# All of the planner's free choices to VectorE, and an early call for the first two attention weights

## The chip, the cores and the metric

The kernel runs on one core of a Trainium2 chip. The metric is the device time of one execution in microseconds. The engines are named as the profile names them: PE is TensorE (PEld its weight loads), DVE is VectorE, ACT is ScalarE, POOL is GpSimd, SP is SyncE, which only issues DMAs here. Times of the kernel before: 2492.51 us, median of three runs (2489.13 to 2495.65).

## The reference

One layer of a decoder trunk serves a prompt of 512 tokens and 8 samples of 8 new tokens each with the same weights, all in float32. Cut to what matters:

```python
proj = x @ w_in
u, cq, ckv_raw, kr_raw = jnp.split(proj, [1024, 1536, 2048], axis=-1)
y_ssm, h_last = s5_group(u, h0, p)                       # state scan, then GLU
q = (rms_norm(cq, g_q) @ w_uq).reshape(b, s, 8, 192)     # 128 plain + 64 rotary per head
q_lat = einsum('bshn,rhn->bshr', q[..., :128], w_uk)
q_rope = apply_rope(q[..., 128:], pos)
ckv, krope = rms_norm(ckv_raw, g_kv), apply_rope(kr_raw, pos)
o_lat = attend(q_lat, q_rope, ckv, krope)                # causal, or over 1024 cached rows
y_att = einsum('bshr,rhv->bshv', o_lat, w_uv)
x = layer_norm(alpha * x + concat([y_ssm, y_att]) @ w_out)
x = layer_norm(alpha * x + (silu(x @ w_gate) * (x @ w_up)) @ w_down)
```

## The kernel before, in words

All 576 tokens (512 of the prompt, 64 of the samples) are the moving columns of the matmuls, in two halves of 288. Weights and activations are split into a high part, rounded to a shorter format, and a low part, the rest; a product is three matmuls: high by high, high by low, low by high (`mm3`, `mmx`). A split (`split`) is a copy to the high part on ACT and a subtraction for the low part on DVE or POOL. So each weight that PE uses passes a DMA, ACT and then DVE or POOL; `wraw`, `whi` and `wlo` are its three tiles. `Ring` loads and splits the weights in the order of a list, two ahead; `weights` makes the list that begins with the prompt attention, and its first two entries are the value and key halves of `w_kv`.

The stages: the input projection with the S5 parameters, states, taps and state scan beside it (`in_proj`, `s5_side`; to about 312 us); the first queries (`to_heads`, `rope_queries`, `nope_queries`) and the prompt attention (`prompt_phase`, to about 500); the sample attention over the cached pages together with the output projection, the residual sums `z` and the first layer norm (`sample_phase`, `out_phase`, `norm1`); the FFN, whose gate, up and most of whose down products use a form of fast matrix multiplication with 7 products for 8 (`ffn_phase`; from about 890); the second layer norm (`norm2`) on the last sums.

A layer norm of one half runs in three steps. `shift` subtracts a rough mean from each of 16 blocks `z`; `moments` adds up blocks and squares (the accumulators lie in `m`, `QS` or, in the last norm, in `xl`); `normed` takes pairs of blocks, 576 columns, subtracts the mean, multiplies by the reciprocal deviation, and scales and shifts each block on ACT or DVE, whichever the planner holds free earlier.

The order of the instructions on each engine is made while the program is built. The class `Clock` keeps a planned end time for every engine and tile, the generators (fibers) of the stages are advanced by these times (`merge`), and a scheduler then orders the instructions by priority (`cur_priority`) and its own timeline. `sooner` is the place where the plan chooses between DVE and POOL for one elementwise operation: it takes POOL where the planned end there is more than 500 ns before the planned end on DVE. It serves the low parts of `split` from SBUF, the sums of `rope`, the low parts of the rotary queries, the low parts of the cached pages (`pages`: `ckthi` and `cktlo` for scores, `cknlo` for values), and `shift`, `moments` and `normed`. Some work is written for POOL outright and stays there: the taps' powers `P` and `PX` and the states' products `Gx`, `Gy` in the S5 stage, copies of query columns, the sum of high and low part in `gates`, and DMAs that accumulate into `pa`.

Of the kernel before, what the change touches and what calls it, by code (L numbers as in the profile page):

```python
# [162 lines left out]
class Clock:  # L163
# [98 lines left out]

    def sooner(self, op, out, *ins):

        t = self.ready(*ins)
        d, p = (max(t + 150, self.end[e]) + self.cost(e, op, out, ins) for e in ('DVE', 'POOL'))
        return self.gpsimd if p + 500 < d else self.vector

    def note(self, eng, op, a, k, r):
        aps = [x for x in list(a) + list(k.values()) if hasattr(x, 'tensor') and hasattr(x, 'dtype')]  # L270
# [249 lines left out]
class Layer:  # L520
# [228 lines left out]
    def weights(self):  # L749

        io = self.io
        cut = lambda w: [w[:, :1024], w[:, 1024:]]
        items = []
        for pr in range(4):
            kv = cut(io['w_kv'][pr])
            lat = cut(io['w_ukt'][pr // 2])[pr % 2:pr % 2 + 1]
            items += cut(io['w_uq'][pr])[::-1] + kv[:1] + lat + kv[1:] if pr else kv[::-1] + lat
        items += [io['w_glu'][m] for m in range(8)]
        mix = [[cut(io['w_out'][m])[i] for m in range(KD)] for i in range(2)]
        items += mix[1] + mix[0]  # L760
        for m in range(8, KD):
            if m in VALUES:
                items.append(io['w_kv'][VALUES.index(m)][:, 1024:])
            items.append(mix[0][m])
        items += mix[1]
        for n in range(2 * HEADS):
            items += [io['w_gu'][n // 2, n % 2, 2 * r:2 * r + 2, :, :512].rearrange("q p c -> p q c") for r in range(2)]
        self.ring = Ring(self, self.wst, "w", 1024, items, ahead=100)

    def place(self, j):  # L770

        j -= 16
        if j < 2:
            return None
        if j == 2:
            hi, lo = self.ff.tile([128, 1024], F32R, name="E"), self.cst.tile([128, 1024], F32R, name="rp")
            return [[x[:, 256 * i:256 * i + 256] for x in (hi, lo)] for i in range(4)]
        if j == 3:
            return [list(x) for x in zip(self.t4[:4], self.t4[4:])]
        a, b = (('T2', 'B22'), ('B11', 'B21'))[j // 2 - 2]  # L780
        k = j % 2 * 2
        return self.X[a][k:k + 2] + self.X[b][k:k + 2]
# [1673 lines left out]
```

## Time and profile before

| | us |
|---|---|
| median of three runs | 2492.51 (2489.13 to 2495.65) |
| profiled execution, its own time | 2493.54 |
| its span, first to last instruction | 2491.5 |
| PE busy | 2350.2 (94%) |
| DVE busy | 1957.2 (79%), 3313 instructions |
| ACT busy | 1077.4 (43%), 1685 instructions |
| POOL busy | 444.4 (18%), 390 instructions |
| mean granted clock of PE | 0.969 |

An engine's busy time is the time covered by its instructions; two that overlap by their pipeline are not counted twice. A granted clock of 1.00 is 2.4 GHz and 0.50 is 1.2 GHz; a mean between them tells which share of a stretch ran at the lower level. In the timeline, idle time ahead of an instruction stands in brackets with what ended it.

### The profile page before, as it was taken

How to read it: one execution, taken by the hardware profiler on the slowest of the kernel's cores; microseconds unless marked ns; L12 is line 12 of the kernel's file. 1: busy time of each engine (PE TensorE's matmuls, PEld its weight loads, DVE VectorE, ACT ScalarE, POOL GpSimd, SP SyncE). 2: the span in 40 equal slices, each digit the busy share in tenths (PEclk: the TensorE clock that was granted, in tenths of full speed). 3: DMA queues.
4: the chain of work that ended last, by engine and by line, in shares of the span. 5: the costliest groups of instructions: out<-in, count | busy, mean ns of one | idle time of the engine just before them, and what ended most of it. 6: DMA issues, size and time to landing. Idle time of an engine off the chain costs nothing.

```text
span 2491.5 us, 45005 instructions
## 1 busy us (share of the span) xinstructions
PE 2350.2 (94%) x17220; PEld 2297.1 (92%) x17220; DVE 1957.2 (79%) x3313; ACT 1077.4 (43%) x1685; POOL 444.4 (18%) x390
## 2 busy tenths in 40 slices
PE   8988989999899989999999999999999999979995
PEld 7877989998898989999999999999999999979994
DVE  7759766778778886999988878887778876755978
ACT  4221355656555544433333333333336644553133
POOL 2682010143344550000000000000000000000335
PEclk9988999999999989999999999999999999989997
DMA  6563456478765556455433333333236765677622
GB/s 216 178 183 120 105 161 199 144 240 294 243 194 165 198 172 217 174 183 190 164 113 132 120 113 132 112 123 107 107 113 208 254 186 143 170 205 251 243 94 76
DMA packets 219161, 419.90 MB, mean 169 GB/s; under 512 B 62210, under 2 KB 127106, under 8 KB 217154
## 3 DMA queue, kind: packets, MB, share of 16 engines
q1 hardware_dynamic: 187154, 359.66, 43.5%
q10 hardware_dynamic: 30064, 44.98, 5.0%
q0 software_dynamic: 1728, 12.39, 2.8%
q8 instruction: 135, 2.21, 0.4%
q14 instruction: 80, 0.66, 0.1%
HBM read 337.52 MB, written 83.64 MB: 169 GB/s over the span
## 4 chain that ended last, share of the span: by engine, by line
PE 56%; DVE 12%; DMA 11%; issue 3%; ACT 3%; POOL 1%; SPq 0%; ACTq 0%; DVEq 0%; POOLq 0%
PE mm L180 34%; PE sc L180 21%; DVE wlo L180 3%; DVE z L180 2%; DVE xl L180 2%; DMA wraw<-w_gu 2%; DMA hraw<-hd 1%; PE po L180 1%; DMA cktraw<-ckt 1%; DMA mraw<-so 1%; DVE T L180 1%; ACT whi L180 1%; DMA T<-pa 1%; DVE Al L180 1%; DVE g L180 1%
## 5 line engine op out<-in xcount | busy, mean ns | idle before, releaser
L180 PE MATMUL mm<-xh,whi 128*128 128x288 f32 x2272 | 606.1, 305 | 17.5 <-ACT xh L180 9.6
L180 PE MATMUL mm<-xh,wlo 128*128 128x288 f32 x2272 | 607.1, 304 | 13.6 <-DVE wlo L180 13.3
L180 PE MATMUL mm<-xl,whi 128*128 128x288 f32 x2272 | 605.7, 303 | 4.5 <-DVE xl L180 4.0
L180 PEld LDWEIGHTS mm<-xh,whi 128*128 128x128 f32 x2272 | 409.8, 193 | 26.8 <-ACT xh L180 10.9
L180 PEld LDWEIGHTS mm<-xh,wlo 128*128 128x128 f32 x2272 | 410.6, 193 | 20.9 <-DVE wlo L180 18.0
L180 PEld LDWEIGHTS mm<-xl,whi 128*128 128x128 f32 x2272 | 411.1, 193 | 7.8 <-DVE xl L180 5.0
L180 PE MATMUL sc<-z,whi 128*128 128x288 f32 x1470 | 350.8, 297 | 1.2 <-ACT z L180 0.6
L180 ACT ACTIVATE whi<-wraw 128x1024 fp32r<-128x1024 f32 (+2 forms) x159 | 173.8, 1094 | 281.1 <-PE mm L180 187.2
L180 DVE TENSOR_TENSOR wlo<-wraw,whi 128x1024 fp32r<-128x1024 f32 (+2 forms) x150 | 214.4, 1431 | 89.7 <-ACT whi L180 87.4
L180 ACT ACTIVATE whi<-E 128x1024 fp32r<-128x1024 f32 x120 | 127.2, 1060 | 334.7 <-issue 193.1
L180 PEld LDWEIGHTS sc<-z,whi 128*128 128x128 f32 x1470 | 250.7, 189 | 2.3 <-ACT whi L180 1.0
L180 ACT ACTIVATE whi<-rp 128x1024 fp32r<-128x1024 f32 x120 | 127.4, 1061 | 256.9 <-issue 191.3
L180 DVE TENSOR_TENSOR wlo<-E,whi 128x1024 fp32r<-128x1024 f32 x120 | 146.7, 1223 | 94.0 <-ACT whi L180 93.5
L180 POOL DMA_DIRECT2D pa<-m x6 | 5.3, 890 | 1200.2 <-ACT m L180 1200.2
L180 PE MATMUL mm<-T,H 128*128 128x288 f32 x1200 | 217.3, 296 | 1.8 <-ACT T L180 1.7
L180 DVE TENSOR_TENSOR wlo<-rp,whi 128x1024 fp32r<-128x1024 f32 x120 | 146.5, 1221 | 72.1 <-ACT whi L180 71.9
L180 PEld LDWEIGHTS mm<-T,H 128*128 128x128 f32 x1200 | 180.8, 189 | 2.5 <-ACT T L180 2.2
L180 PE MATMUL mm<-Ah,wlo 128*128 128x288 f32 x480 | 137.5, 308 | 14.6 <-DVE wlo L180 12.7
L180 PE MATMUL sc<-Ah,H 128*128 128x288 f32 x552 | 144.3, 297 | 6.6 <-DVE H L180 3.2
L180 PE MATMUL mm<-Ah,H 128*128 128x288 f32 x552 | 144.4, 297 | 4.2 <-ACT Ah L180 4.2
L180 PE MATMUL sc<-z,wlo 128*128 128x288 f32 x490 | 145.8, 298 | 0.9 <-DVE wlo L180 0.9
L180 PE MATMUL sc<-g,whi 128*128 128x288 f32 x490 | 144.8, 295 | 0.9 <-ACT g L180 0.8
(505 smaller groups left out, 5493.6 us busy)
## 6 DMA issues: line engine op xcount, KB each, us to landing
wraw<-w_gu SPq DMA_DIRECT2D x145, 512.0 KB, 3.2
qns<-w_gu SPq DMA_DIRECT2D x59, 512.0 KB, 3.3
wraw<-w_out SPq DMA_DIRECT2D x56, 512.0 KB, 3.9
wraw<-w_dq SPq DMA_DIRECT2D x43, 512.0 KB, 3.4
cktraw<-ckt SPq DMA_DIRECT2D x64, 320.0 KB, 4.5
cknraw<-ckn SPq DMA_DIRECT2D x64, 256.0 KB, 3.9
hd<-QS ACTq DMA_DIRECT2D x16, 1008.0 KB, 4.1
wraw<-w_in SPq DMA_DIRECT2D x14, 1024.0 KB, 5.8
```

What stands on the lines that cost most here:

```text
L180: r = f(*a, **k)
```

## The change

`sooner` no longer compares; it returns DVE. And behind the weight list of the prompt attention, the ring is asked at once to load and split its first two entries, with a priority that is moved 400 ahead of the place reached.

```diff
     def sooner(self, op, out, *ins):
 
-        t = self.ready(*ins)
-        d, p = (max(t + 150, self.end[e]) + self.cost(e, op, out, ins) for e in ('DVE', 'POOL'))
-        return self.gpsimd if p + 500 < d else self.vector
+        return self.vector
...
         self.ring = Ring(self, self.wst, "w", 1024, items, ahead=100)
 
+        at = self.tc.cur_priority
+        self.tc.cur_priority = max(at - 400, 0)
+        self.ring.split(1)
+        self.tc.cur_priority = at
```

What this makes of the order is seen in three places. The first is ACT where the first queries end and the prompt attention begins. `rt` and `qrh` are rotary parts of the first queries, `qnh` their plain parts, `kr` the rotary key; `whi<-wraw` twice is the pair of weights. Before:

```order
L180 ACTIVATE rt<-mm 32x576 x4
L180 ACTIVATE qnh<-mm 128x576
L180 ACTIVATE kr<-rva 128x576
L180 DMA o_kr<-rva 64x576
L180 ACTIVATE qnh<-mm 128x576
L180 ACTIVATE qrh<-qr 64x576 x4
L180 ACTIVATE whi<-wraw 128x1024 x2
```

The same place now:

```order
L180 ACTIVATE rt<-mm 32x576 x4
L180 ACTIVATE qnh<-mm 128x576
L180 ACTIVATE kr<-rva 128x576
L180 DMA o_kr<-rva 64x576
L180 ACTIVATE qnh<-mm 128x576
L180 ACTIVATE qrh<-qr 64x576 x4
L180 ACTIVATE whi<-wraw 128x1024 x2
```

Nothing moved there: the pair follows the four copies `qrh` in both.

The second place is DVE where the first norm of the second half has its statistics (`RECIPROCAL QS`) and the first FFN weights are split beside it; `g` and `z` are the pairs of blocks, `QS` holds mean and reciprocal deviation. Before:

```order
L180 RECIPROCAL QS<-QS 96x3
L180 TENSOR_TENSOR wlo<-wraw,whi 128x1024
L180 TENSOR_TENSOR xres<-xres,mm 128x288
L180 TENSOR_TENSOR z_10035<-z_10035,QS 128x576 x2
L180 TENSOR_SCALAR z_10035<-z_10035,vec 128x288
L180 TENSOR_TENSOR wlo<-wraw,whi 128x1024
L180 TENSOR_TENSOR xl_212<-z_10035,xh_196 128x576
```

Now:

```order
L180 RECIPROCAL QS<-QS 96x3
L180 TENSOR_TENSOR wlo<-wraw,whi 128x1024
L180 TENSOR_TENSOR xres<-xres,mm 128x288
L180 TENSOR_TENSOR g_7372<-g_7372,QS 128x576
L180 TENSOR_TENSOR z_10035<-z_10035,QS 128x576
L180 TENSOR_TENSOR g_7373<-g_7373,QS 128x576
L180 TENSOR_TENSOR z_10036<-z_10036,QS 128x576
L180 TENSOR_TENSOR g_7372<-g_7372,QS 128x576
L180 TENSOR_TENSOR z_10035<-z_10035,QS 128x576
L180 TENSOR_TENSOR g_7373<-g_7373,QS 128x576
L180 TENSOR_TENSOR wlo<-wraw,whi 128x1024
```

Seven of the eight pairs were POOL's with both steps and came to DVE; seven steps now stand ahead of the next low part `wlo`, where two stood.

The third place is DVE at the end of the program, from the last reciprocal on; `xh_26921` holds the second half's mean and deviation, `xh_26917` the first half's. Before:

```order
L180 RECIPROCAL xh_26923<-xh_26923 96x3
L180 TENSOR_SCALAR Ah_26659<-Ah_26659,vec 128x288 x2
L180 TENSOR_TENSOR z_26646<-z_26646,xh_26921 128x576
L180 TENSOR_TENSOR z_26648<-z_26648,xh_26921 128x576
L180 TENSOR_TENSOR Al_26656<-Al_26656,xh_26921 128x576
L180 TENSOR_TENSOR z_26646<-z_26646,xh_26921 128x576
L180 TENSOR_TENSOR g_26650<-g_26650,xh_26921 128x576
```

Now:

```order
L180 TENSOR_TENSOR Ah_26657<-Ah_26657,xh_26917 128x576
L180 TENSOR_TENSOR z_26646<-z_26646,xh_26921 128x576
L180 TENSOR_TENSOR z_26648<-z_26648,xh_26921 128x576
L180 TENSOR_TENSOR g_26650<-g_26650,xh_26921 128x576
L180 TENSOR_TENSOR z_26652<-z_26652,xh_26921 128x576
L180 TENSOR_TENSOR Al_26654<-Al_26654,xh_26921 128x576
L180 TENSOR_TENSOR Al_26656<-Al_26656,xh_26921 128x576
L180 TENSOR_TENSOR Al_26658<-Al_26658,xh_26921 128x576
L180 TENSOR_TENSOR Al_26660<-Al_26660,xh_26921 128x576
L180 TENSOR_TENSOR Ah_26659<-Ah_26659,xh_26917 128x576
L180 TENSOR_TENSOR z_26646<-z_26646,xh_26921 128x576
L180 TENSOR_TENSOR z_26648<-z_26648,xh_26921 128x576
```

The differences of all eight pairs of the second half now stand on DVE ahead of their products, with late steps of the first half's pairs `Ah` around them; five of the differences were POOL's.

## Rows read from the trace of the kernel before

**Rows 1.** Stretches: us, busy us of PE, PEld, DVE, ACT, POOL, clock, DMA

```profile
500.00:880.00 380.00, 356.87 (x2426) 337.83 (x2425) 303.07 (x460) 212.38 (x333) 171.96 (x125) 0.95 0.68 222
880.00:935.00 55.00, 44.96 (x306) 44.25 (x305) 47.54 (x51) 26.07 (x41) 29.39 (x19) 0.88 0.53 173
935.00:1870.00 935.00, 930.25 (x6971) 926.89 (x6970) 776.02 (x1194) 350.36 (x456) 0.00 (x0) 1.00 0.40 140
2305.00:2430.00 125.00, 120.62 (x894) 118.86 (x893) 108.13 (x164) 31.20 (x58) 45.70 (x33) 1.00 0.46 167
2430.00:2491.50 61.50, 31.04 (x204) 29.57 (x203) 51.94 (x77) 21.63 (x45) 31.59 (x19) 0.76 0.23 77
```

**Rows 2.** PE's waits, whole span: us in total, times, longest

```profile
PE mm L180 <- DVE wlo L180: 26.0, 17, 6.9
...
PE mm L180 <- POOL P L180: 7.9, 3, 5.1
```

**Rows 3.** DVE by form, 935 to 1870 us: count, busy us, mean ns, idle before

```profile
L180 DVE TENSOR_TENSOR wlo<-E,whi 128x1024 fp32r<-128x1024 f32 x87 | 106.4, 1223 | 65.0 <-ACT whi L180 64.5
...
L180 DVE TENSOR_TENSOR QS<-QS,mm 128x576 f32<-128x576 f32 x35 | 26.2, 749 | 4.4 <-PE mm L180 4.1 <-issue 0.2
```

**Rows 4.** DVE by form, 500 to 935 us

```profile
L180 DVE TENSOR_TENSOR wlo<-wraw,whi 128x1024 fp32r<-128x1024 f32 x77 | 109.0, 1416 | 24.7 <-ACT whi L180 24.3
...
L180 DVE TENSOR_TENSOR z<-z,mm 128x288 f32<-128x288 f32 x24 | 10.7, 447 | 10.0 <-PE mm L180 10.0
```

**Rows 5.** DVE by form, 880 to 935 us

```profile
L180 DVE TENSOR_TENSOR wlo<-wraw,whi 128x1024 fp32r<-128x1024 f32 x12 | 19.0, 1582 | 6.1 <-ACT whi L180 6.1
L180 DVE TENSOR_SCALAR g<-g,vec 128x288 f32<-128x288 f32 x5 | 6.0, 1222 | 0.0
...
L180 DVE TENSOR_TENSOR z<-z,QS 128x576 f32<-128x576 f32 x2 | 3.4, 1715 | 0.1
L180 DVE TENSOR_TENSOR m<-g,z 128x576 f32<-128x576 f32 x2 | 2.7, 1352 | 0.0
```

**Rows 6.** POOL by form, 500 to 935 us

```profile
L180 POOL TENSOR_TENSOR ckthi<-cktraw,ckthi 64x256 fp32r<-64x256 f32 x30 | 41.6, 1389 | 60.7 <-ACT ckthi L180 49.2 <-PE mm L180 4.5 <-PE po L180 4.2
...
L180 POOL TENSOR_TENSOR g<-g,QS 128x576 f32<-128x576 f32 x8 | 16.2, 2040 | 8.6 <-ACT QS L180 8.6
...
L180 POOL TENSOR_TENSOR z<-z,QS 128x576 f32<-128x576 f32 x6 | 10.1, 1699 | 0.0
```

**Rows 7.** Timeline of DVE near 917 us: start, us

```profile
915.72 1.95 DVE L180 TENSOR_TENSOR m<-m,z 128x576 f32<-128x576 f32 x1
917.58 2.42 DVE L180 TENSOR_TENSOR wlo<-wraw,whi 128x1024 fp32r<-128x1024 f32 x1
```

**Rows 8.** Timeline of PE from 901.5 to 921 us

```profile
904.94 0.40 PE L180 MATMUL mm<-Ah,wlo 128*128 128x288 f32 x1 [2.73 <-DVE wlo L180]
...
920.06 0.61 PE L180 MATMUL mm<-Ah,wlo 128*128 128x288 f32 x1 [6.93 <-DVE wlo L180]
```

**Rows 9.** DVE by form, 2430 us to the end

```profile
L180 DVE TENSOR_TENSOR z<-z,xh 128x576 f32<-128x576 f32 x7 | 11.1, 1590 | 0.8 <-ACT xh L180 0.7
```

**Rows 10.** Timeline of DVE, last 21 us

```profile
2471.23 2.63 DVE L180 TENSOR_TENSOR z<-z,xh 128x576 f32<-128x576 f32 x2 [0.74 <-ACT xh L180]
2473.78 1.95 DVE L180 TENSOR_TENSOR Al<-Al,xh 128x576 f32<-128x576 f32 x1
...
2482.94 2.08 DVE L180 TENSOR_TENSOR Al<-Al,xh 128x576 f32<-128x576 f32 x3
2485.06 0.43 DVE L180 TENSOR_SCALAR Al<-Al,vec 128x288 f32<-128x288 f32 x1
```

**Rows 11.** Timeline of ACT, last 21 us

```profile
2486.05 1.13 ACT L180 ACTIVATE Al<-Al,vec 128x288 f32<-128x288 f32 x2
```

**Rows 12.** Timeline of ACT at the first attention weights

```profile
316.97 2.00 ACT L180 ACTIVATE whi<-wraw 128x1024 fp32r<-128x1024 f32 x2
```

**Rows 13.** Timeline of PE at the first attention weights

```profile
318.08 0.38 PE L180 MATMUL mm<-whi,xh 128*128 128x256 f32 x1 [4.66 <-ACT whi L180]
```

## The prediction

> **What bounds the kernel now.** I read the stretches first [rows 1]: us of each stretch, busy us of TensorE (PE), of its weight loads, of VectorE (DVE), ScalarE (ACT) and GpSimd (POOL), then the granted clock. From 935 to 1870 us PE is busy 930 of 935 at clock 1.00 and POOL does nothing: nothing moved here, nothing to win. In the other four stretches POOL works, PE falls short of its stretch, and in three of them the clock is under 1.00. There DVE is the busiest engine beside PE: 303 of 380 us, 47.5 of 55, 108 of 125, and 51.9 of the last 61.5, where PE has only 31. Of PE's waits [rows 2] the largest is for wlo, the low part of a weight, made by DVE; another is for P, made by POOL.
>
> Then one operation, with and without POOL beside it. In the stretch without POOL a 1024-wide low part takes 1223 ns and a 576-wide sum 749 ns [rows 3]. From 500 to 935 the same low part takes 1416 ns on average over 77, while a sum that reads one operand from PSUM stays at 447 ns [rows 4]. From 880 to 935, where the second half's normalisation runs on POOL, the low part takes 1582, a 576-wide product 1715, a 288-wide scale-and-shift 1222 (alone 0.43 us [rows 10]) [rows 5]. So DVE stands still while POOL holds something both need, and an operation that POOL does in 1.4 to 2.0 us [rows 6] costs DVE much of the time that it was to save.
>
> **The change part by part.** The order of the changed kernel has 199 instructions fewer on POOL and 183 more on DVE: the 199 arrive, and 16 scale-and-shifts (`normed` picks the engine that the planner believes free) go over to ACT. No instruction is added or dropped. An instruction's time on DVE is taken from a stretch without POOL: 0.75 us for 576 columns [rows 3], 0.45 for 288, since the sum from PSUM is of that size [rows 4]; 0.69 and 0.42 for 512 and 64x256 are estimates between these by their columns. The sum is made against the profiled execution's 2493.5 us, 1.0 above the median of 2492.5.
>
> *First weights split early: 0.* PE ends the first queries and waits 4.66 us [rows 13] for the pair of high parts, which ACT starts at 316.97 [rows 12] behind the queries' own parts. In the order after the change the pair stands in the same place on ACT and on DVE; only buffer numbers differ. So the wait stays. Bounds: 0, and -3.5 if the pair were really to start as PE ends (313.4). I take 0.
>
> *Start and S5, to 312 us: -3.* Twelve low parts (eight 576, four 512 wide) come to DVE at some 0.75 and 0.69: 8.8 us, while twelve POOL spans go. PE waited 7.9 us for P [rows 2]. In the new plan the first of those products stands in the same column block, but ten k steps (60 matmuls, some 8 us) later, and the other seven follow with it. That can remove the first wait (5.1) and part of the second; the remaining S5 work of POOL, and DVE's lengthening beside it, stay as they are. Between -7.9 (all of it) and +4 (the products come late for the state scan), I take -3, nearer to the small end because the wait may only move.
>
> *Sample attention and mixing, 500 to 880: -3.* POOL's 125 instructions [rows 1] less the 14 sums for the gates, which stay, are 111: 30 rotary low parts of 64x256 at about 0.42, 11 of 512 at 0.69, 62 of 288 at 0.45, 8 of 576 at 0.75. That is 54 us for DVE. Against it stands what DVE gets back: 77 low parts lose 0.19 each up to 935 [rows 4], 14.9 us, the other forms that ran beside POOL as much again and more. So DVE's load hardly changes, but each moved result is ready about 1 to 1.3 us sooner than on POOL [rows 6]. PE is idle 23 us here and the clock of 0.95 is worth another 19; most of it hangs on loads and ACT too. Ends: -12, and +8 if DVE, which takes its work strictly in turn, now has shifts and norms ahead of low parts. I take -3.
>
> *Second half's normalisation and the first FFN heads, 880 to 935: -5.* Here PE stands still 2.73 and 6.93 us for wlo [rows 8], and the wlo that ends the second wait took 2.42 us itself, behind a queue of operations at more than twice their length [rows 7]. Relief by the groups of [rows 5]: 12 x 0.36 + 5 x 0.80 + 2 x 0.97 + three groups of m (one is shown), 6 x 0.60 = 13.8 us. Added: the fourteen 576-wide differences and products [rows 6], 14 x 0.75 = 10.5. Net -3.3, and some scale-and-shifts go to ACT, which is busy 26 of 55. In the new order seven products stand ahead of the next wlo instead of two, 7 x 0.67 = 4.7 us (without POOL one starts 0.67 after another: three in 2.08 [rows 10]), so the first wait shrinks by a microsecond or two; of the second I expect to see less than half. The pace lost while the clock stood at half (0.88 over the stretch) comes back in part. Ends: -11 (both waits, and 1.3 of what the clock took), 0 (the waits move to loads of w_gu). I take -5.
>
> *End, 2305 to the last instruction: -5.* In the last 61.5 us DVE is busy 52, PE 31: DVE sets the end. Relief: z 7 x 0.84 [rows 9], 5.9 us, and by the sums in xl and the smaller groups of that answer some 13 more. Added: POOL's 19 [rows 1], all 576 wide, 14.3. Net about -4, and some scale-and-shifts fewer, though they reappear on ACT. The very last piece gains nothing: from the mean's arrival at 2471.2, DVE took differences at 1.95 beside POOL and was done at 2485.5 [rows 10]; now eight differences and eight products at 0.67 are done after 11 us, but all 16 scale-and-shifts are ACT's, 16 x 0.52 behind the first product: again some 16 us, as before (2487.2 [rows 11]). So the gain must come before 2471, where the squares and sums were slowed: 4, and one more from 2305 to 2430, where DVE is busy 108 of 125 and PE 121. Ends: -9 and +2 (five output DMAs queue behind ACT's last instruction, about 0.4 each). I take -5.
>
> Sum: 0 - 3 - 3 - 5 - 5 = -16; 2493.5 - 16 = 2477.5 for the profiled execution, about 2477 for the median.
>
> **The rivals.** *Relief, but off the path (2487).* PE is 94% busy, its waits are short and many, and a wait for wlo can turn into one for the weight's load or for ACT, which gets 16 instructions more. Then only the end's 5 us remain. For it: the plan is another from the first microsecond on, and even the largest kind of wait is 17 waits with 26 us together [rows 2]. Against it: the last stretch and the one of [rows 8] are DVE's own.
>
> *DVE overloaded (2509).* If DVE's long operations are long for another reason (the transfers of those stretches, say), nothing comes back and the added time is real: 303 + 54 = 357 of 380 us, 47.5 + 10.5 = 58 of 55, 51.9 + 14.3 = 66 of 61.5. That is 3 + 5 us over the stretches' lengths, and at 94% load in strict order I price the first at another 8: +16. It decides where a wlo from 500 to 935 fails to fall back from 1416 to about 1223. Against it: the 447 ns of [rows 4], in the same stretch with the same transfers. The Trainium skill (Perfetto Trace Analysis, Optimizing Scalar/DVE Operations) says that with a saturated DVE it may make sense to move work to ScalarE or even GpSimd; undoing that would be this case, and by it alone the time would be near 2509. The same section warns that the two share a read port of SBUF, so that moving between them may not help; the rows above bear out the warning, not the advice.
>
> *The early split does act (2474).* If the pair ran as soon as PE ended, 3.5 us more would go. The order speaks against it.
>
> **How the numbers follow.** Forecast 0.62, off the path 0.24, overload 0.11, early split 0.03. The forecast's own range runs over the ends of the terms taken together in part: 2461 to 2485. Reaching to the second case's middle and some way beyond, 2461 to 2496 leaves out the overload and a little on each side. A measurement tells 0.3% (7.5 us) from no change: faster means under 2485.0, slower over 2500.0. Faster 0.62 + 0.03 = 0.65, same 0.24, slower 0.11.
>
> **What would show it.** Right: in the changed profile wlo from 500 to 935 takes 1.22 to 1.25 us, the 576-wide operations of normalisation 0.75, POOL is busy some 155 us and idle after 560 except for copies and accumulating DMAs; DVE's total stays within 30 us of 1957; the two waits of [rows 8] sum to under 6; the wait of 4.66 at the first weights is still there; the stretch from 935 to 2250 is as long as before. Wrong: DVE over 95% busy from 560 to 880 with PE waiting for cknlo, cktlo or z (overload); equal waits under other names (off the path); new waits for P or for the scan before 312 us.

## The result and the profile after

The changed kernel takes **2459.58 us** (median of four runs, 2451.82 to 2464.12) against 2491.36 for the kernel before in the same measurement: ratio **0.9863**, 95% interval 0.9845 to 0.9881. Some 32 to 34 us are gained where about 16 were forecast; the time lies just under the forecast range. The profiled execution took 2464.12 us, its span is 2462.0 (before 2491.5). The page's line of engine totals:

```profile
PE 2335.2 (95%) x17220; PEld 2283.0 (93%) x17220; DVE 1938.6 (79%) x3496; ACT 1085.5 (44%) x1701; POOL 163.1 (7%) x191
```

VectorE has 183 instructions more than before and is busy 19 us less. The stretches, with the columns of [rows 1]; the last three are bounded by the two reciprocals of the last normalisation (first half's, second half's) and the end:

```profile
500.00:880.00 380.00, 356.72 (x2460) 336.62 (x2458) 309.63 (x558) 216.43 (x343) 11.65 (x10) 0.96 0.68 224
880.00:935.00 55.00, 48.64 (x353) 46.59 (x352) 52.55 (x80) 32.16 (x49) 0.00 (x0) 1.00 0.65 210
935.00:1870.00 935.00, 930.55 (x6971) 926.83 (x6970) 775.57 (x1202) 350.03 (x461) 0.00 (x0) 1.00 0.39 138
2290.00:2414.00 124.00, 121.66 (x900) 120.98 (x899) 105.20 (x207) 32.72 (x61) 0.00 (x0) 0.99 0.44 161
2414.00:2441.00 27.00, 22.04 (x163) 21.75 (x162) 22.87 (x55) 13.63 (x28) 0.00 (x0) 0.94 0.19 66
2441.00:2462.00 21.00, 2.36 (x12) 2.12 (x10) 13.85 (x22) 11.08 (x22) 0.00 (x0) 0.50 0.41 140
```

Behind 543 us GpSimd has only its accumulating DMAs left. From 500 to 880 us VectorE does 98 instructions more than in [rows 1] in 6.6 us more. VectorE by form, 500 to 935 us:

```profile
L180 DVE TENSOR_TENSOR wlo<-wraw,whi 128x1024 fp32r<-128x1024 f32 x80 | 97.6, 1220 | 20.5 <-ACT whi L180 20.1
...
L180 DVE TENSOR_TENSOR z<-z,mm 128x288 f32<-128x288 f32 x24 | 10.8, 448 | 2.9 <-PE mm L180 2.7
...
L180 DVE TENSOR_TENSOR z<-z,QS 128x576 f32<-128x576 f32 x8 | 6.0, 752 | 0.0
L180 DVE TENSOR_TENSOR g<-g,QS 128x576 f32<-128x576 f32 x8 | 6.0, 752 | 0.0
```

The low part falls from 1416 ns [rows 4] to 1220, the time that it had without GpSimd [rows 3]; the sum with an operand in PSUM stays at 448. The last two forms were GpSimd's, at 1699 and 2040 ns [rows 6]. Waits of PE, summed, and its timeline at the places of [rows 13] and [rows 8]:

```profile
PE mm L180 <- DVE wlo L180: 23.2, 18, 8.3
...
PE mm L180 <- POOL P L180: 6.1, 1, 6.1
```

```profile
311.25 0.48 PE L180 MATMUL mm<-whi,xh 128*128 128x256 f32 x1 [4.66 <-ACT whi L180]
...
891.61 0.40 PE L180 MATMUL mm<-Ah,wlo 128*128 128x288 f32 x1 [1.31 <-DVE wlo L180]
900.28 0.40 PE L180 MATMUL mm<-Ah,wlo 128*128 128x288 f32 x1 [1.92 <-DVE wlo L180]
```

The waits of 2.73 and 6.93 us are now 1.31 and 1.92; the 4.66 us at the first attention weights are still there to the hundredth. The largest gain of one stretch stands between the last normalisation's two reciprocals. VectorE's timeline, before and then after:

```profile
2431.87 0.17 DVE L180 RECIPROCAL xh<-xh 96x3 f32<-96x3 f32 x1
...
2469.66 0.17 DVE L180 RECIPROCAL xh<-xh 96x3 f32<-96x3 f32 x1
```

```profile
2414.12 0.17 DVE L180 RECIPROCAL xh<-xh 96x3 f32<-96x3 f32 x1
...
2440.98 0.17 DVE L180 RECIPROCAL xh<-xh 96x3 f32<-96x3 f32 x1
```

37.8 us became 26.9. From the second reciprocal to the end it was 21.8 and is 21.0.

Where the span's 29.5 us came from by engine: the idle times ahead of all 17,220 matmuls add up to 122.8 us before and 108.2 after (-14.6); the mean granted clock rose from 0.969 to 0.974, and (1 - 0.969) x 2491.5 less (1 - 0.974) x 2462.0 is 13. So by this reckoning (the mean clock counts PE's idle stretches too) nearly half of the gain is less time at the lower of PE's two levels, not shorter waits themselves. PE's busy time says the same without the clock: the same 17,220 matmuls took 2350.2 us before and 2335.2 after (-15.0). By place, from starts of the same instructions in both traces (us; one execution each):

| | before | after | gained so far |
|---|---|---|---|
| first product with attention weights | 318.1 | 311.3 | 6.8 |
| first scores of the sample attention | 500.8 | 497.4 | 3.4 |
| third product of the sample values (sc<-olh) | 783.5 | 781.7 | 1.8 |
| reciprocal of the second half's first normalisation | 894.3 | 882.7 | 11.6 |
| end of the FFN heads (14th xres sum) | 999.7 | 980.3 | 19.4 |
| last normalisation, first half's reciprocal | 2431.9 | 2414.1 | 17.8 |
| last normalisation, second half's reciprocal | 2469.7 | 2441.0 | 28.7 |
| end | 2491.5 | 2462.0 | 29.5 |

(`olh` holds the high and low parts of the sample attention's outputs.) Such starts shift by several us between executions of one order: the heads' end stands at 978.1 to 983.6 us in the four kernels of this document whose PE order is the same (the changed one and, below, e1, e3, e4). So a term is read between two neighbouring rows, and the medians below decide. One stretch is the same in every kernel of this document: between the last two reciprocals lie 37.8 us wherever the old choice stands there, and 26.8 or 26.9 wherever the planner gives all of the last normalisation to VectorE (e3, with work added beside it, apart).

### The profile page after: what moved, and what is told of

It reads as the page before. It is cut to its first block, busy times and chain, and to the rows that moved or that the text cites. A ratio compares the mean times of both kernels' runs of the same rounds, so it can differ in the third digit from the quotient of the medians.

```text
span 2462.0 us, 44884 instructions
## 1 busy us (share of the span) xinstructions
PE 2335.2 (95%) x17220; PEld 2283.0 (93%) x17220; DVE 1938.6 (79%) x3496; ACT 1085.5 (44%) x1701; POOL 163.1 (7%) x191
## 4 chain that ended last, share of the span: by engine, by line
PE 64%; DMA 10%; DVE 8%; ACT 3%; issue 2%; SPq 0%; ACTq 0%; DVEq 0%
PE mm L180 39%; PE sc L180 23%; DVE wlo L180 2%; PE po L180 2%; DMA wraw<-w_gu 2%; ACT whi L180 1%; DMA xres<-hd 1%; DVE z L180 1%; DMA mraw<-so 1%; DMA cktraw<-ckt 1%; DMA mraw<-hd 1%; DMA wraw<-w_dq 1%; DMA hraw<-hd 1%; DVE g L180 1%; DMA wraw<-w_out 1%
## 5 line engine op out<-in xcount | busy, mean ns | idle before, releaser
L180 PE MATMUL mm<-xh,wlo 128*128 128x288 f32 x2272 | 605.1, 303 | 14.9 <-DVE wlo L180 14.6
L180 PEld LDWEIGHTS mm<-xh,whi 128*128 128x128 f32 x2272 | 408.4, 193 | 30.4 <-ACT xh L180 10.1
L180 DVE TENSOR_TENSOR wlo<-wraw,whi 128x1024 fp32r<-128x1024 f32 (+2 forms) x159 | 204.2, 1285 | 74.9 <-ACT whi L180 74.4
L180 PE MATMUL sc<-g,wlo 128*128 128x288 f32 x490 | 144.3, 294 | 0.0
```

What stands on the lines that cost most here:

```text
L180: r = f(*a, **k)
```

## Experiments

Theory A: VectorE stands still while GpSimd reads operands from the same memory, and the change removes that. Theory B: the gain is the planner's new order. Theory C: the early split earns a part. Ratios are to the kernel before in the same measurement.

**e1: everything on VectorE, no early split.**

```diff
-        self.ring.split(1)
```

> The changed kernel without its second part: everything on VectorE, no early split call. Theory A (the gain is VectorE no longer standing still beside GpSimd) and theory B (the gain is the other order that the planner finds): the time of the changed kernel, 2460 us within 4, ratio to before 0.985 to 0.989; the wait of 4.66 us at the first attention weights as in the changed kernel. Theory C (the early split call earns part of it): 3.5 us more than the changed kernel, 2463 or above, and that wait 3 us longer.

2459.99 us, ratio 0.9853 (0.9828 to 0.9879). The first product with attention weights starts at 311.2 us behind the same wait of 4.66. C falls: the early split earns nothing, and the instruction order with and without it is the same but for buffer numbers.

**e2: the old plan, carried out on VectorE.** The planner's clock goes on reckoning with GpSimd; only the engine that gets the instruction is another. The scheduler behind it still sees the true engine, so the order is near the old one, not equal to it.

```diff
+        self.noted = Clock.Engine(self, 'POOL', nc.vector)
-        return self.gpsimd if p + 500 < d else self.vector
+        return self.noted if p + 500 < d else self.vector
```

> The planner decides and reckons as before, GpSimd included, but what it gives to GpSimd is issued on VectorE. Theory A (VectorE stands still beside GpSimd): most of the gain is there although the plan is the old one, 2460 to 2472 us, and a 1024-wide low part from 500 to 935 us takes 1.22 to 1.25 us instead of 1.42. Theory B (the gain comes from the planner's new order): within 0.3 per cent of the kernel before, or slower, since VectorE gets work that its plan doesn't know of: 2485 to 2510 us.

2466.43 us, ratio 0.9886 (0.9866 to 0.9906), beside 0.9853 for e1. By the medians over three quarters of the gain (0.0114 of 0.0147; the two intervals overlap) come without the planner knowing of the change, and the low part is as short:

```profile
L180 DVE TENSOR_TENSOR wlo<-wraw,whi 128x1024 fp32r<-128x1024 f32 x80 | 97.7, 1221 | 18.3 <-ACT whi L180 17.4
```

A holds, B's numbers fall; a plan that knows the truth may be worth the rest. Between the last two reciprocals it shows: 31.8 us in e2, 26.9 after the change, 37.8 before. There 6 of the 10.9 us come with the old plan and the other 5 only with the new one, which also has more of the scale-and-shifts on ACT (1701 ACT instructions, 1685 in e2); 1.5 of those 5 e2 has back behind the second reciprocal (19.5 us to the end, 21.0 after the change).

A rival to A isn't tested by a run of its own: that GpSimd's slow results simply came late for those who needed them. The trace of the kernel before speaks against it. On the chain that ended last GpSimd has 1%:

```profile
PE 56%; DVE 12%; DMA 11%; issue 3%; ACT 3%; POOL 1%; SPq 0%; ACTq 0%; DVEq 0%; POOLq 0%
```

The largest waits of PE for it are 7.9 us for P, which the change leaves on GpSimd, and 2.9 for `cknlo`.

**e3 and e4: GpSimd reads, or only writes, beside the same VectorE work.** Both are e1 with useless work on GpSimd in the last normalisation; VectorE's, ACT's and PE's orders are e1's.

```diff
+                nc.gpsimd.tensor_copy(scr[:, :8], self.m[0][1][:, :8])
+                for _ in range(20):
+                    nc.gpsimd.tensor_tensor(scr, c, c, OP.add)
```

e4 has 50 times `nc.gpsimd.memset(scr, 0.0)` in the place of the 20 sums.

> The vector-only kernel plus 20 useless sums of 288 columns on GpSimd (they read constants, nobody waits for them), begun when the first half's last mean and scale arrive. Orders of the other engines are the same. Theory A: VectorE's products and differences of 576 columns beside them go from 0.75 to 1.4 to 1.7 us, the time between the two reciprocals of the last normalisation rises from 27 us to 33 to 38, and the kernel takes 6 to 11 us more than the vector-only one. Theory B: 0 to 1 us more, all operations as long as without.

> The same with 50 fills of 288 columns on GpSimd, which read nothing, in the place of the 20 sums. Theory A, in the form that it is GpSimd's reading of operands that VectorE's operations wait for: 576-wide operations stay at 0.75 us, 27 to 28 us between the two reciprocals, the vector-only kernel's time within 1.5 us. Rival form (any work of GpSimd on the same memory stops VectorE): like the sums, operations of 1.2 us and more and 5 us or more lost.

VectorE by form, 2414 to 2446 us, of e3, then of e4, and GpSimd's useless work from 2400 to 2470 in the last line of each:

```profile
L180 DVE TENSOR_TENSOR z<-z,xh 128x576 f32<-128x576 f32 x6 | 5.7, 986 | 0.6 <-ACT xh L180 0.6
...
L180 DVE TENSOR_TENSOR xl<-xl,Al 128x288 f32<-128x288 f32 x8 | 4.6, 577 | 0.0
...
L180 DVE TENSOR_TENSOR Al<-Al,sc 128x288 f32<-128x288 f32 x4 | 1.8, 441 | 0.0
...
L180 POOL TENSOR_TENSOR mraw<-c 128x288 f32<-128x288 f32 x20 | 17.6, 882 | 1.6
```

```profile
L180 DVE TENSOR_TENSOR z<-z,xh 128x576 f32<-128x576 f32 x6 | 4.3, 752 | 0.6 <-ACT xh L180 0.6
...
L180 DVE TENSOR_TENSOR xl<-xl,Al 128x288 f32<-128x288 f32 x8 | 3.6, 450 | 0.0
...
L180 DVE TENSOR_TENSOR Al<-Al,sc 128x288 f32<-128x288 f32 x4 | 1.8, 447 | 0.3 <-PE sc L180 0.3
...
L180 POOL MEMSET mraw<- 128x288 f32 x50 | 16.9, 338 | 2.9
```

Nearly the same GpSimd time, 17.6 and 16.9 us. Over this stretch, operations with both operands in SBUF take 0.99 in place of 0.75 and 0.58 in place of 0.45 us beside the sums; the one with an operand in PSUM keeps its 0.44. Beside the fills nothing changes. These means mix in operations outside the sums' own 19 us (2418.0 to 2437.1); well inside them 576-wide operations take 0.85 or 1.22 us, and 288-wide ones 0.55 or 0.92; two of the first:

```profile
2424.11 1.22 DVE L180 TENSOR_TENSOR z<-z,xh 128x576 f32<-128x576 f32 x1
...
2427.23 1.22 DVE L180 TENSOR_TENSOR z<-z,xh 128x576 f32<-128x576 f32 x1
```

Between the two reciprocals lie 32.5 us in e3 (2413.25 to 2445.78) and 26.8 in e4, against 26.9 after the change. So A holds in mechanism and place; its size was set too high (32.5 where 33 to 38 were expected, 1.22 where 1.4 to 1.7 were). The medians don't separate the two from each other or from e1 (2466.59 and 2465.38, e1 2459.99; the three intervals overlap): e4 has 5 us more too, with nothing lengthened. In the traces those 5 us aren't the fills': e4's first reciprocal stands at 2418.0, e1's at 2413.4, and e4's first fill comes at 2422.8. In e3 the first reciprocal is e1's (2413.3), and the 5.5 us by which its span is longer all lie behind it. The Trainium skill (SBUF — State Buffer, Who interferes with whom) states this rule: a VectorE instruction with two SBUF inputs contends with a GpSimd instruction that reads SBUF, and not with one that only writes. These two runs agree.

**s1 to s4, m1 to m3: the stages by themselves and together.** A flag lets `sooner` return VectorE alone in some of four stages; elsewhere the old rule stands.

```diff
+        if self.alone:
+            return self.vector
         t = self.ready(*ins)
```

> VectorE alone in the input projection, S5 and the first queries (to 312 us); the old choice after that; no early split. If the stages add up: the first attention weights' product begins 7 us sooner than before, at 311 us, and later landmarks stand about as far ahead; 2484 to 2488 us by the kernel before's 2491. Rival (the lead of 7 us is lost where the sample attention waits for its loads): the second half's normalisation begins within 2 us of before's and the time is before's within 2 us.

> VectorE alone from the prompt attention to the end of the sample attention and the first products of the mixing (312 to 780 us); the old choice elsewhere; no early split. If the stages add up: 0 to 5 us lost or gained between the first weights and the sample values' products, since VectorE takes 54 us of work and gets back much the same: 2487 to 2496 us. Rival (VectorE's relief pays here as it does at the end): 5 us or more gained, 2486 or less.

> VectorE alone from the sample values' products through the second half's normalisation to the end of the FFN's main part (780 to 2390 us); the old choice elsewhere; no early split. If the stages add up: the fourteenth xres sum (the heads' end) stands 8 to 12 us ahead of before's, the last stretch is as long as before, 2480 to 2484 us. Rival (the plan's order did it): 2489 or more.

> VectorE alone from the second part of the FFN on (the last normalisation); the old choice before it; no early split. If the stages add up: until 2390 us as before; 26 to 28 us between the two reciprocals of the last normalisation in place of 38; 2479 to 2483 us. Rival (the gain at the end needs the earlier stages' order): under 4 us gained.

> VectorE alone from the prompt attention to the end of the FFN's main part (312 to 2390 us), the old choice in the start and in the last normalisation; no early split. VectorE alone from 312 to 780 us by itself had cost 31 us, from 780 to 2390 us by itself had gained 6. Theory A1 (those 31 us are paid behind 780 us, where GpSimd comes back beside VectorE that then has the first half's normalisation, low parts and sums to do at once): they are gone here, 10 to 20 us gained, 2473 to 2483 us, and from the sample values' first product to the heads' end 197 to 210 us as in the changed kernel (199), not 229. Rival A2 (VectorE is overloaded from 312 to 780 us itself): about the sum of both, 2510 to 2520 us.

> VectorE alone everywhere except from 312 to 780 us, where the old choice between VectorE and GpSimd stays; no early split. If moving the sample attention's work to VectorE is worth nothing or costs something (in the kernel with VectorE alone in the start, the sample values began at 771 us, 10 us ahead of the changed kernel): 2448 to 2460 us. If that move is needed for the later gain, as theory A1 has it from the other side: only the parts that gained by themselves, 6 and 10, remain, 2472 to 2480 us.

> VectorE alone from 780 us to the end, the old choice before that; no early split. The start's share is what m2 (which has the start as well) is faster than this one. If the start's lead of 7 us is kept to the end when the stretch behind 780 us has no GpSimd: 2464 to 2468 us here, against 2458 there. If the stages' own gains only add (6 and 10): 2475 to 2480, and the start is worth 17 to 20 us in company, more than its own lead. If the start's lead is lost even then: 2457 to 2461.

| VectorE alone in | median us | ratio, 95% interval |
|---|---|---|
| s1: start | 2493.94 | 1.0004, 0.9992 to 1.0016 |
| s2: sample attention | 2524.92 | 1.0131, 1.0107 to 1.0155 |
| s3: second half's normalisation, heads | 2487.50 | 0.9971, 0.9958 to 0.9985 |
| s4: tail | 2483.33 | 0.9955, 0.9937 to 0.9973 |
| m1: sample, second | 2496.12 | 1.0009, 0.9999 to 1.0019 |
| m3: second, tail | 2474.76 | 0.9910, 0.9889 to 0.9930 |
| m2: start, second, tail | 2458.41 | 0.9852, 0.9833 to 0.9872 |
| e1: all four | 2459.99 | 0.9853, 0.9828 to 0.9879 |

Alone, the four add to a loss of some 15 us; together they gain some 37 (the ratios times 2494). Second half and tail do add (7 and 11 us by their ratios; m3's 0.9910 is 22, its interval 17 to 28). The start gains nothing alone and some 14 us beside them (0.9852 against 0.9910; 4 to 24 by their intervals): in s1 its first product with attention weights starts at 310.5 us, and from the sample values (the landmark in the table above) to the heads' end, with GpSimd, 224 us pass, against 216 before and 208 in m2. The sample attention is worth nothing beside the others (m2 and e1), and costs 31 us alone. In m2's trace the nothing is two parts that cancel: with GpSimd its sample attention takes 277 us from the first scores to the sample values, after the change 284; behind them m2 needs 208 us to the heads' end, the changed kernel 199. Of what s2 loses, one part shows from 780 to 1000 us: from the sample values to the heads' end 229 us pass, 13 more than before. The stretch of s2, of the kernel before and of the changed one:

```profile
780.00:1000.00 220.00, 181.30 (x1193) 175.82 (x1192) 161.12 (x204) 97.00 (x159) 87.90 (x61) 0.86 0.50 159
```

```profile
780.00:1000.00 220.00, 201.57 (x1400) 196.58 (x1400) 178.57 (x236) 106.15 (x175) 84.08 (x56) 0.93 0.58 191
```

```profile
780.00:1000.00 220.00, 207.38 (x1484) 202.07 (x1483) 177.76 (x302) 112.47 (x186) 0.00 (x0) 0.97 0.58 191
```

The waits of PE in s2 in that stretch:

```profile
PE mm L180 <- DVE wlo L180: 24.1, 10, 5.2
PE sc L180 <- DVE olh L180: 6.6, 1, 6.6
PE sc L180 <- DVE o L180: 2.6, 1, 2.6
```

With GpSimd back beside VectorE, PE gets 291 matmuls fewer done there than in the changed kernel, at clock 0.86. In m1, where no GpSimd follows, the heads' end comes 199 us after the sample values, as after the change (A1's number), but the time is before's: A1 is right for the part behind the sample values and wrong on the sum. The other part of the loss lies ahead, in m1 and s2 alike: the sample attention takes 296 us from the first scores to the sample values (before 283, after 284), with PE standing 5.0 and 2.9 us in m1, 6.6 and 2.6 in s2, for `olh` and `o`, the attention's outputs, at its end. That is A2's place, but not A2's size. Both have the old start; after the change `olh` keeps PE 0.7 us. Why the plan after the old start leaves PE without other products there was not tried.

**b1, b2, b3: S5's products too.** In both kernels GpSimd keeps S5's products from 62 to 250 us, and VectorE's operations are still long there. b2 moves the two products for the states, b1 all of S5's 97 sums and products, b3 in addition issues five stores on GpSimd's queue.

```diff
-        pt = nc.gpsimd.tensor_tensor
+        pt = nc.vector.tensor_tensor
...
-                nc.sync.dma_start(self.Sd[64 * r:64 * r + 64, g2::2, 1:PC], S[64 * g2:64 * g2 + 64, :, r, :PC - 1])
+                nc.gpsimd.dma_start(self.Sd[64 * r:64 * r + 64, g2::2, 1:PC], S[64 * g2:64 * g2 + 64, :, r, :PC - 1])
```

> As the one before, but only the 16 products of S5's states (Gx, Gy) go to VectorE; the taps' products stay on GpSimd. VectorE gets 11 us of work and loses the lengthening beside 23 us of GpSimd's. Theory A: the first attention weights' product begins 1 to 5 us sooner than 311 us, 2454 to 2459 us. Rival (no relief, since GpSimd starts the taps earlier instead): within 1 us of 311 us, the vector-only kernel's time.

> The vector-only kernel with S5's products and sums for the states and taps on VectorE too (97 instructions, which GpSimd has in both kernels). Theory A: VectorE's 46 us of lengthening from 62 to 250 us go, about 53 us of work come, and each P is ready some 2 us sooner; of PE's waits for P, wlo and rssq (6.1, 8.4, 3.0 and 6.5 us) some go: the first attention weights' product begins 4 to 12 us sooner than 311 us, the kernel takes 2448 to 2456 us. Rival (VectorE becomes the bound of this stretch): the first weights' product 5 to 15 us later than 311 us, 2465 us or more.

> As S5 on VectorE, but the stores of the states (Sd, four, and o_sp) are issued on GpSimd's queue, not on SP's, where in that kernel the first two attention weights' loads stand behind them and are issued at 286.5 us while PE waits 12.1 us. If that queue is what PE waits for there: the wait at the first attention weights falls to 4 to 6 us (what ACT's own order leaves), 2441 to 2446 us. Rival (the loads wait for room in memory, or the stores take longer on the other queue and the states come late): the wait stays over 10 us or a new one for H stands behind it, 2449 us or more.

b2: 2459.12 us, ratio 0.9850 (0.9830 to 0.9870), which can't be told from e1's; the first product with attention weights stands at 309.5 us, 1.7 sooner, so b2 decides nothing. b1: 2449.65 us, ratio 0.9813 (0.9796 to 0.9829); that product at 294.4 us, 17 sooner than after the change, more than expected. VectorE by form and the stretch from 62 to 250 us, after the change and in b1:

```profile
L180 DVE TENSOR_TENSOR wlo<-wraw,whi 128x2048 fp32r<-128x2048 f32 x10 | 25.7, 2566 | 1.6 <-ACT whi L180 1.6
...
62.00:250.00 188.00, 156.22 (x1342) 149.24 (x1341) 157.25 (x327) 42.34 (x53) 112.28 (x102) 0.90 0.49 150
```

```profile
L180 DVE TENSOR_TENSOR wlo<-wraw,whi 128x2048 fp32r<-128x2048 f32 x12 | 27.5, 2290 | 0.0
...
L180 DVE TENSOR_TENSOR P<-P,PX 128x576 f32<-128x576 f32 x16 | 12.2, 760 | 0.0
...
62.00:250.00 188.00, 174.63 (x1530) 169.14 (x1529) 162.36 (x434) 47.49 (x59) 1.23 (x6) 0.95 0.52 160
```

VectorE does 107 instructions more in 5.1 us more, and PE 188 matmuls more. The wait at the first attention weights, 4.66 us after the change, takes part of it back; PE there and SP's queue in b1:

```profile
294.37 0.58 PE L180 MATMUL mm<-whi,xh 128*128 128x256 f32 x1 [12.11 <-ACT whi L180]
```

```profile
271.16 6.90 SPq L180 DMA_DIRECT2D Sd<-S  x3
278.10 5.73 SPq L180 DMA_DIRECT2D o_sp<-so  x1
283.87 1.17 SPq L180 DMA_DIRECT2D Sd<-S  x1
286.53 2.37 SPq L180 DMA_DIRECT2D wraw<-w_kv  x2
```

In b3 the two loads are issued at 263.2 us, and the same matmul reads:

```profile
292.60 0.58 PE L180 MATMUL mm<-whi,xh 128*128 128x256 f32 x1 [8.69 <-ACT whi L180]
```

The wait falls to 8.7, not to the 4 to 6 expected: ACT has its four copies of the first queries' rotary parts ahead of `whi`, as in every kernel here, and is done with them at 291.5 us, while PE stands from 283.9. b3 takes **2444.57 us**, ratio **0.9791** (0.9777 to 0.9805), the fastest of all, ahead of both kernels.

## Why the prediction was wrong in size

**The mechanism was right.** Low parts at 1220 ns, 576-wide operations at 752, GpSimd busy 163 us (155 forecast), VectorE's total 19 us under before's (within 30 of it was forecast), the two waits of [rows 8] at 3.2 together, the wait of [rows 13] unchanged, 935 to 2250 us as long as before: each sign named beforehand is there. The rival of an overloaded VectorE fell with the low part. The rival in which relief stays off the path fell with m3 and m2. The early split acts in no trace; e1 shows it.

**The step that failed is the sum's sizes**, -3 -3 -5 -5. By the landmarks above, which don't lie exactly on the terms' bounds, the same four are -6.8, -4.8, -7.8 and -10.1: every term too small by a factor of 1.6 to 2.3, each inside its bounds but the end's. In e1's trace, of the same order, they are -6.9, -4.9, -6.4 and -12.0.

- *End, -5 taken.* 1.6 us were lost between the heads' end and the first of the last two reciprocals, 10.9 gained between the two, 0.8 behind. I set a relief of 5.9 and some 13 us against nineteen operations of 0.75 us (14.3) and got a net 4. The answer that holds [rows 9] gives more; its next groups, 288 columns wide, 0.45 us without GpSimd, 0.42 for `vec`:

```profile
L180 DVE TENSOR_TENSOR xl<-xl,xh 128x288 f32<-128x288 f32 x10 | 7.8, 782 | 0.4 <-ACT xh L180 0.3
...
L180 DVE TENSOR_TENSOR xl<-xl,xl 128x288 f32<-128x288 f32 x5 | 4.7, 939 | 0.0
L180 DVE TENSOR_TENSOR xl<-xl,z 128x288 f32<-128x288 f32 x4 | 3.9, 970 | 0.0
L180 DVE TENSOR_SCALAR z<-z,vec 128x288 f32<-128x288 f32 x3 | 3.0, 1001 | 0.0
```

  The groups beside the 5.9 add up to 14.9, and nine scale-and-shifts leave VectorE for ACT there (22 on ACT before, 31 after; 9 x 0.42 = 3.8). So the same sum comes to 5.9 + 14.9 + 3.8 - 14.3 = 10.3 in place of 4. That it meets the 10.1 so closely is partly luck: it counts VectorE's time and not the chain's, and e1's trace has 12.0. The stretch of the kernel before between its two reciprocals:

```profile
2432.00:2470.00 38.00, 26.70 (x180) 25.71 (x179) 35.36 (x56) 12.67 (x26) 22.13 (x14) 0.90 0.14 47
```

  VectorE had 56 instructions there in 35.4 us, beside 14 of GpSimd; after the change it has 55 in 22.9. The mean fell from 0.63 to 0.42 us, and the count didn't rise, in part since ACT has those scale-and-shifts: the term named them and did not subtract them. That the last piece gains next to nothing was right. s4 has the term by itself: 0.9955, 11 us.
- *Second half's normalisation and first heads, -5 taken, -7.8 measured.* The two waits of [rows 8] gave 6.4 of 9.7 us, as forecast. But the stretch runs at clock 1.00 in place of 0.88, which is 6.6 of its 55 us at the full level; I let that come back only in part. The two can't be added up, since the mean clock counts PE's standing too: between the landmarks (894.3 to 999.7, 882.7 to 980.3) PE stands 4.4 us less and is busy 3.4 less.
- *Start, -3 taken, -6.8 measured*, and found again in every kernel with a start on VectorE alone and S5 as it was (that landmark at 310.5 to 312.1 us, against 315.7 to 319.9 with the old start). I took the small end because the wait for P might only move; it did shrink little (7.9 to 6.1 us). What carries the rest of the lead isn't settled: in these two traces it is PE's busy time for the same 2176 matmuls (275.0 to 268.9 us; standing 43.1 to 42.4), in the others mostly the standing (43 to 49 us with the old start, 39 to 44 with the new).
- *Sample attention and mixing, -3 taken, -4.8 measured*, but as the sum of a loss and a gain: 5.0 lost up to the sample values (3.4 of them ahead of the first scores, outside the term's stretch), 9.8 won in the mixing behind them, where [rows 6] had GpSimd's norms. e1 against m2 says that the attention's part is worth nothing.

**The sum's form failed too.** I added stages as if each kept its own gain. The start is worth 0 or 14 us, the sample attention costs 31 or nothing, by which other stages have GpSimd beside VectorE. And I priced mostly waits, while about 13 of 29 us are the clock. Measured apart, the two parts whose gain does repeat are the end's (the 37.8 and 26.9 above) and the second half's normalisation (from its reciprocal to the heads' end 97 to 101 us in every kernel without GpSimd there, 105 to 113 with it).

## What to carry to other kernels

Before giving GpSimd a share, compare one form's duration on VectorE with and without GpSimd beside it, apart for operands in SBUF and in PSUM: where the first grows and the second doesn't, set that growth against what the move saves. This planner's `cost` has no such term: it reckons a 576-wide operation on VectorE at 0.67 us whatever GpSimd does, and the trace has 0.75 without GpSimd and 1.72 beside it [rows 5]. Look for the work left there too: here the last 97 such operations were worth another 10 us. Price a stage's relief in the company of the later stages, and count the clock at the lower level beside the waits.

## What the runs showed that was not expected

- GpSimd's fills, 50 in 16.9 us, left VectorE's operations at 0.75 and 0.45 us; its sums, 20 in 17.6 us, took them to 0.85 or 1.22 and to 0.55 or 0.92 while they ran.
- One stage moved alone made the kernel 31 us slower, and cost nothing once the others were moved.
- In b1 three stores of the scan's states held SP's queue for 6.9 us and the next for 5.7, with the loads that PE waited for behind them.
